# SSD output of a hybrid SSD/MLA step: y scaled group by group, and the order of three GpSimd products in two scan groups

## The chip, the cores and the metric

The kernel runs on one core of one Trainium2 chip. The metric is device time in microseconds (us). The core has five engines that work side by side, each through its own instructions in order: TensorE (PE in the profile; its weight loads are listed as PEld), VectorE (DVE), ScalarE (ACT), GpSimd (POOL) and SyncE (SP), which issues most of the transfers. They wait for each other by semaphores.

## The reference

One step of a two-layer decoder trunk: a Mamba-2 SSD layer, then a latent-attention layer, over a prompt of 1024 tokens and 8 × 8 sample tokens. The change lies in the SSD layer. There a projection gives z, x, B, C and dt; x, B and C go through a causal convolution and SiLU; then come the chunked scan, the skip product, the gate, a normalisation over each of 8 groups of 256 channels, and the output projection:

```python
def ssd_scan(x, dt, a_head, bm, cm, init_state):
    ...
    y_diag = jnp.einsum('bgrcls,bcsgrp->bclgrp', cb[:, :, None] * decay, xdt)
    decay_end = jnp.exp(a_cs[..., -1:] - a_cs).transpose(0, 3, 4, 1, 2)
    states = jnp.einsum('bcsgn,bcsgrp->bcgrpn', bc, xdt * decay_end[..., None])
    ...
    def step(s, inp):
        st, dec = inp
        return dec[..., None, None] * s + st, s
    ...
    y_off = jnp.einsum('bclgn,bcgrpn->bclgrp', cc, prev) * decay_in[..., None]

def ssd_mixer(...):
    ...
    y = y + d_skip.astype(F32)[:, None] * xs
    y = y.reshape(b, t, SSD_D_INNER) * jax.nn.silu(z.astype(F32))
    yg = y.reshape(b, t, SSD_GROUPS, SSD_D_INNER // SSD_GROUPS)
    yg = yg * lax.rsqrt(jnp.mean(yg * yg, axis=-1, keepdims=True) + NORM_EPS)
    y = yg.reshape(b, t, SSD_D_INNER) * norm_w.astype(F32)
    out = jnp.einsum('bte,ed->btd', y.astype(h.dtype), w_out)
```

## The kernel before

All numbers are float32. To keep their precision on TensorE, most operands are split in two: a high part, which ACT makes by a rounding copy, and a low part, the **remainder**, value minus high part, which DVE or POOL makes. A product is then three matmuls (high × high, high × low, low × high). `split` (L125) issues the two instructions; its subtraction is on POOL where POOL is passed, and it returns that last instruction.

**Groups.** The SSD layer goes over the 8 channel groups. While group g is scanned (`ssd_scan`, L733, which interleaves `ssd_chunks` and `ssd_states`), the projection, convolution and gate of group g+1 are issued beside it (L926 to L938). The last group, g = 7, has no next group: beside its scan stands the first half of the output projection (L949 to L953).

**A chunk.** `ssd_chunks` (L580) takes nine tiles of tokens, eight chunks of 128 prompt tokens and one of 64 sample tokens. For each prompt chunk:
- PE transposes x and B; ACT copies x out as xsT.
- POOL multiplies xsT by the decay to the chunk's end: xdd (L613). `split` makes xddh (ACT) and xddl (POOL, L615, listed under L133).
- From the second chunk on, C and the state S are split too (L617 to L620).
- POOL multiplies xsT by the skip weight: xD (L622).
- The 128x512 matrix M of decays is loaded by SP (L626), masked on DVE (L627), exponentiated on ACT (L630) and multiplied by C·B on DVE (L631); PE multiplies it with xsT into py (L635).
- PE adds Bh·xddh, Bh·xddl, Bl·xddh into st (L639), in that order; from C and S it makes the state's part of py (L644).
- POOL decays the state, S2 = S × decay (L645); DVE adds st to it (L647).
- DVE and POOL join y from py, xD (L653) and z; ACT squares it into xD, whose buffer is reused (two buffers); SP stores y (L658).

**The states of the sample.** `ssd_states` (L669) treats the 8 × 8 sample tokens; its line L713 splits a transposed state, and the remainder, called sl, is made on DVE and used by PE at L719.

**The output projection.** `OutHalf.prep` (L801) loads one tile of y with four groups (1024 columns), multiplies each group's 256 columns by that group's norm factor (L812), transposes it on PE (L820) four blocks at a time, and splits it. `ssd_out` (L832) does the matmuls. The first half (tiles named yta, poa; groups 0 to 3) runs beside the scan of group 7; the second (ytb, pob; groups 4 to 7) after it. There are nine tiles in each half.

**What sets the order.** In this layer the program gives the dependences, and a planner orders each engine's instructions at build time by a timeline of its own; an engine then works through its list strictly in order. `k.tc.issue_after(ins)` makes the instructions traced in its block, on the same engine as `ins`, stand behind `ins` in that list. The attention layer's PE and POOL lists are written out by hand (`manual_schedule`, L1999 and L2003). Transfers on SP's queue are in order too.

Of the kernel before, what the change touches and what calls it, by code (L numbers as in the profile page):

```python
# [11 lines left out]
ALU = mybir.AluOpType  # L12
# [15 lines left out]
G = 8  # L28
# [54 lines left out]
def mm3(nc, out, pairs):  # L83
    n = len(pairs)
    for i, (a, b) in enumerate(pairs):
        nc.tensor.matmul(out, a, b, start=(i == 0), stop=(i == n - 1))  # L86
# [38 lines left out]
def split(k, hi, lo, src, eng=None, parts=0):  # L125
    nc = k.nc
    nc.scalar.copy(hi, src)  # L127
    n = parts and hi.shape[1] // parts
    for a in range(parts):
        s = slice(a * n, a * n + n)  # L130
        (eng or nc.vector).tensor_tensor(lo[:, s], src[:, s], hi[:, s].bitcast(F32), op=ALU.subtract)
    if not parts:
        return (eng or nc.vector).tensor_tensor(lo, src, hi.bitcast(F32), op=ALU.subtract)  # L133
# [446 lines left out]
def ssd_chunks(k, gr, pools):  # L580
    nc, I = k.nc, k.I
    sp, psum = pools
    g = gr.g
    S = None
    hs = slice(4 * g, 4 * g + 4)
    for i in range(9):
        t0, m = TILES[i]
        sl = slice(t0, t0 + m)
        smp = i == 8
        B, C, X0, X1 = (gr.xc[q][1][:, j] if smp else gr.xc[q][0][:, j, sl] for q in range(2) for j in range(2))  # L590
        z = gr.z[i // 5][:m, i % 5]
        tag = f"{g}_{i}"
        p = psum.tile([128, 512], F32, tag="tr", name="trp" + tag, bufs=PB["tr"])
        nc.tensor.transpose(p[:m, 0:128], X0, k.ident)
        nc.tensor.transpose(p[:m, 128:256], X1, k.ident)
        if not smp:
            nc.tensor.transpose(p[:m, 256:384], B, k.ident)
        xsT = sp.tile([128, 256], F32, tag="xsT", name="xsT" + tag, bufs=2)
        nc.scalar.copy(xsT[:m], p[:m, 0:256])  # L599
        if not smp:  # L600
            Bh, Bl = (sp.tile([128, 128], F32R, tag="BT" + x, name="BT" + x + tag, bufs=2) for x in "hl")
            split(k, Bh, Bl, p[:, 256:384])
        tk = k.tok[:m, i]

        def hb(j):
            return tk[:, j, hs].unsqueeze(2).to_broadcast([m, 4, 64])

        def v3(t):
            return t[:m].rearrange("p (h q) -> p h q", q=64)

        if not smp:
            xdd = sp.tile([128, 256], F32, tag="xdd", name="xdd" + tag, bufs=1)
            nc.gpsimd.tensor_tensor(v3(xdd), v3(xsT), hb(2), op=ALU.mult)  # L613
            dh, dl = (sp.tile([128, 256], F32R, tag="xdd" + x, name="xdd" + x + tag, bufs=1) for x in "hl")
            split(k, dh, dl, xdd, nc.gpsimd)  # L615
            if S is not None:
                Ch, Cl = (sp.tile([128, 128], F32R, tag="C" + x, name="C" + x + tag, bufs=1) for x in "hl")  # L617
                split(k, Ch, Cl, C, nc.gpsimd)
                Sh, Sl = (sp.tile([128, 256], F32R, tag="S" + x, name="S" + x + tag, bufs=1) for x in "hl")
                split(k, Sh, Sl, S, nc.gpsimd)  # L620
        xD = sp.tile([128, 256], F32, tag="xD", name="xD" + tag, bufs=XDB)
        nc.gpsimd.tensor_tensor(v3(xD), v3(xsT), k.dsk[:m, hs].unsqueeze(2).to_broadcast([m, 4, 64]), op=ALU.mult)  # L622
        pc = psum.tile([128, 512], F32, tag="cb", name="cb" + tag, bufs=PB["cb"])
        nc.tensor.matmul(pc[:m, :m], B, C, start=True, stop=True)
        M = sp.tile([128, 4, 128], F32, tag="M", name="M" + tag, bufs=2)
        nc.sync.dma_start(M[:m, :, :m], (k.acss_d[hs] if smp else k.acs_d[i, hs]).partition_broadcast(m))  # L626
        nc.vector.tensor_tensor(M[:m, :, :m], M[:m, :, :m],  # L627
                                (k.negs if smp else k.negu)[:m, :m].unsqueeze(1).to_broadcast([m, 4, m]), op=ALU.add)
        for h in range(4):
            nc.scalar.activation(M[:m, h, :m], M[:m, h, :m], AF.Exp, bias=tk[:, 0, 4 * g + h : 4 * g + h + 1])  # L630
        nc.vector.tensor_tensor(M[:m, :, :m], M[:m, :, :m],  # L631
                                pc[:m, :m].unsqueeze(1).to_broadcast([m, 4, m]), op=ALU.mult)
        py = psum.tile([128, 512], F32, tag="y", name="py" + tag, bufs=PB["y"])
        for h in range(4):
            nc.tensor.matmul(py[:m, h * 64 : h * 64 + 64], M[:m, h, :m], xsT[:m, h * 64 : h * 64 + 64],  # L635
                             start=True, stop=True)
        if not smp:
            ps = psum.tile([128, 512], F32, tag="st", name="st" + tag, bufs=PB["st"])
            mm3(nc, ps[:, :256], [(Bh, dh), (Bh, dl), (Bl, dh)])  # L639
            S2 = sp.tile([128, 256], F32, tag="S", name=f"S{g}_{i + 1}", bufs=2)  # L640
            if S is None:
                nc.vector.tensor_copy(S2, ps[:, :256])
            else:
                mm3(nc, py[:m, 256:], [(Ch, Sh), (Ch, Sl), (Cl, Sh)])  # L644
                nc.gpsimd.tensor_tensor(S2.rearrange("p (h q) -> p h q", q=64), S.rearrange("p (h q) -> p h q", q=64),  # L645
                                        k.decp[:, hs, i : i + 1].to_broadcast([128, 4, 64]), op=ALU.mult)
                nc.vector.tensor_tensor(S2, S2, ps[:, :256], op=ALU.add)  # L647
            S = S2
        y = sp.tile([128, 256], F32, tag="y", name="y" + tag, bufs=YB)
        if i:  # L650
            nc.vector.tensor_tensor(v3(y), v3(gr.yo if smp else py[:, 256:]), hb(3), op=ALU.mult)
            nc.vector.tensor_tensor(y[:m], y[:m], py[:m, :256], op=ALU.add)
            nc.gpsimd.tensor_tensor(y[:m], y[:m], xD[:m], op=ALU.add)  # L653
        else:
            nc.vector.tensor_tensor(y, py[:, :256], xD, op=ALU.add)
        nc.vector.tensor_tensor(y[:m], y[:m], z, op=ALU.mult)
        nc.scalar.activation(xD[:m], y[:m], AF.Square, accum_out=k.yssq[:m, i, g : g + 1])
        nc.sync.dma_start(k.y_d[sl, 256 * g : 256 * g + 256], y[:m])  # L658
        if i == 7:
            pf = psum.tile([128, 512], F32, tag="tr", name="pf" + tag, bufs=PB["tr"])  # L660
            for pr in range(2):
                nc.tensor.transpose(pf[:, pr * 128 : pr * 128 + 128], S[:, pr * 128 : pr * 128 + 128], k.ident)
            fo = sp.tile([128, 256], F32, tag="fo", name="fo" + tag, bufs=1).rearrange("p (a n) -> p a n", a=2)
            nc.scalar.copy(fo, pf[:, :256].rearrange("p (a n) -> p a n", a=2))
            nc.sync.dma_start(k.O["p_ssm"][0, 0, 4 * g : 4 * g + 4].rearrange("(a h) p n -> (h p) a n", h=2), fo)
        yield
# [129 lines left out]
class OutHalf:  # L796
# [4 lines left out]
    def prep(self, i, yp, psum):  # L801
        k, nc, tag, k0 = self.k, self.k.nc, self.tag, self.k0
        nk = NWA
        g0, ng = k0 // 2, nk // 2
        if self.rs is None:
            self.rs = k.cs.tile([128, 9, ng], F32, name="yrs" + tag)
            rstd_of(k, self.rs, k.yssq[:, :, g0 : g0 + ng], 256)
        t0, m = TILES[i]
        y = yp.tile([128, ng, 256], F32, tag="yt", name=f"yt{tag}{i}", bufs=1)
        nc.sync.dma_start(y[:m].rearrange("p g c -> p (g c)"),  # L810
                          k.y_d[t0 : t0 + m, k0 * 128 : (k0 + nk) * 128])
        nc.vector.tensor_tensor(y[:m], y[:m], self.rs[:m, i].unsqueeze(2).to_broadcast([m, ng, 256]), op=ALU.mult)  # L812
        yh = yp.tile([128, nk, 128], F32R, tag="yh", name=f"yh{tag}{i}", bufs=1)
        yl = yp.tile([128, nk, 128], F32R, tag="yl", name=f"yl{tag}{i}", bufs=1)
        yv = y.rearrange("p g c -> p (g c)")
        for q in range(nk // 4):
            p = psum.tile([128, 512], F32, tag="tr", name=f"ytp{tag}{i}{q}", bufs=PB["tr"])
            for a in range(4):
                b = q * 4 + a
                nc.tensor.transpose(p[:, a * 128 : a * 128 + m], yv[:m, b * 128 : b * 128 + 128], k.ident[:m, :m])  # L820
            pv = p.rearrange("p (a t) -> p a t", a=4)[:, :, :m]
            qs = slice(q * 4, q * 4 + 4)
            split(k, yh[:, qs, :m], yh[:, qs, 64:] if m == 64 else yl[:, qs], pv)
        return yh, yl
# [1240 lines left out]
```

## Time and profile before

| what | value |
|---|---|
| three runs | 1943.63, 1947.31, 1948.73 us (median 1947.31) |
| profiled execution | 1942.63 us, its span 1940.9 us |
| granted TensorE clock in it | 0.995 of full speed |
| HBM read and written | 146.52 MB and 53.28 MB |

The profile is of one execution. Rows of a group of instructions give line, engine, operation, output <- inputs, shapes and count, then busy time and mean duration in ns of one, then the idle time of the engine before them and what ended it. Rows of a timeline start with the start in us and the duration in us; in brackets stands the idle time before, with what ended it. Rows of waits give the waiting engine and line, the producer, and total, number and longest. Rows of windows give the length of the stretch, the busy time and number of instructions of each engine, the granted clock, and the share and rate of DMA. A buffer's number is left out of its name, so that xddl is one of several. Matmuls overlap one another: their starts, not their durations, show the rate.

The scale of y takes 1212 to 2876 ns in the first half of the output projection (median 1464, nine instructions) and 1215 to 1227 ns in the second (nine). xD is made 72 times (606 to 1687 ns, median 615), the remainder xddl 64 times (727 to 2266, median 741), the decayed state 56 times (614 to 1803, median 623).

### The profile page before, as it was taken

The page shows a single profiled execution, that of the slowest core. Times are in us where ns is not written, and L with a number is a line of the kernel's source. Part 1 is how long each engine was busy: PE and PEld are TensorE (multiplying, and loading weights), DVE is VectorE, ACT ScalarE, POOL GpSimd, SP SyncE. Part 2 cuts the span into 40 slices and gives each one's busy share as a digit, 9 for nine tenths or more (in the row PEclk, how much of TensorE's full clock was granted, in tenths as well). Part 3 has the DMA queues.
Part 4 walks back from the last instruction along what each step waited for, and adds up shares of the span by engine and source line. Part 5 has one row for each costly group of instructions (what it writes and reads, how often), then busy time and mean ns, then how long its engine had stood idle before and what let it go on. Part 6 is the DMA issues. An engine that isn't in the chain of part 4 may idle for free.

```text
span 1940.9 us, 33581 instructions
## 1 busy us (share of the span) xinstructions
PE 1896.4 (98%) x12023; PEld 1731.9 (89%) x12023; DVE 1191.3 (61%) x2447; ACT 1110.6 (57%) x2535; POOL 844.3 (44%) x1122
## 2 busy tenths in 40 slices
PE   9999999999999999899999999999999999999998
PEld 7999999999999999788787998898888888778887
DVE  5557565756665666765533104466787878676674
ACT  6466676666667676743214314335777777855552
POOL 2447455555655555444003213203443434774551
PEclk9999999999999999999999999999999999999999
DMA  5123323332333332553533333132111112654441
GB/s 165 50 72 87 92 84 98 82 110 82 93 89 93 83 99 66 189 180 133 197 124 109 134 141 91 64 109 89 55 52 41 52 41 59 205 177 154 155 128 39
DMA packets 181087, 202.02 MB, mean 104 GB/s; under 512 B 18828, under 2 KB 147608, under 8 KB 180536
## 3 DMA queue, kind: packets, MB, share of 16 engines
q1 hardware_dynamic: 175864, 180.08, 30.3%
q0 software_dynamic: 4976, 19.66, 3.0%
q8 instruction: 95, 1.56, 0.3%
q14 instruction: 72, 0.59, 0.1%
q10 hardware_dynamic: 80, 0.13, 0.0%
HBM read 146.52 MB, written 53.28 MB: 103 GB/s over the span
## 4 chain that ended last, share of the span: by engine, by line
PE 85%; ACT 4%; DVE 3%; DMA 3%; POOL 2%; issue 1%; SPq 0%; POOLq 0%; DVEq 0%; ACTq 0%
PE pj L86 21%; PE pz L98 8%; PE pq L98 6%; PE pob L98 5%; PE p L98 5%; PE poa L98 5%; PE py L635 2%; PE sc L86 2%; PE o L86 2%; PE sc L1365 2%; PE o L1428 2%; PE o L1430 2%; PE st L1397 2%; PE st L1398 2%; PE st L1399 2%; PE o L1429 2%
## 5 line engine op out<-in xcount | busy, mean ns | idle before, releaser
L86 PE MATMUL pj<-xh,wih 128*128 128x384 f32 (+1 forms) x768 | 254.7, 336 | 0.5 <-ACT raw L512 0.3
L86 PE MATMUL pj<-xl,wih 128*128 128x384 f32 (+1 forms) x768 | 254.1, 331 | 0.0
L86 PE MATMUL pj<-xh,wil 128*128 128x384 f32 (+1 forms) x768 | 253.6, 330 | 0.0
L1411 POOL TENSOR_TENSOR tl<-P,th 128x384 fp32r<-128x384 f32 (+1 forms) x96 | 90.6, 944 | 232.5 <-ACT P L1409 190.9
L526 DVE SCALAR_TENSOR_TENSOR acc<-raw,vec,acc 128x1112 f32<-128x1112 f32 x96 | 141.6, 1476 | 26.5 <-ACT acc L522 25.5
L86 PEld LDWEIGHTS pj<-xh,wih 128*128 128x128 f32 x768 | 144.3, 189 | 2.2 <-ACT xh L273 0.7
L86 PEld LDWEIGHTS pj<-xl,wih 128*128 128x128 f32 x768 | 144.9, 189 | 1.0
L86 PEld LDWEIGHTS pj<-xh,wil 128*128 128x128 f32 x768 | 144.7, 188 | 0.4
L98 PE MATMUL pz<-wih,xh 128*128 128x256 f32 x504 | 142.8, 287 | 0.5 <-ACT z L567 0.5
L98 PE MATMUL pz<-wil,xh 128*128 128x256 f32 (+1 forms) x504 | 140.2, 284 | 0.0
L1408 ACT ACTIVATE th<-st 128x512 fp32r<-128x512 f32 x192 | 94.6, 493 | 65.9 <-PE st L1404 50.3
L98 PE MATMUL pz<-wih,xl 128*128 128x256 f32 x448 | 128.2, 286 | 0.0
L630 ACT ACTIVATE M<-M,tok 128x128 f32<-128x128 f32 (+1 forms) x288 | 90.9, 386 | 64.2 <-DVE M L627 63.8
L1701 POOL TENSOR_TENSOR kvl<-pgr,kvh 128x256 fp32r<-128x256 f32 x128 | 97.6, 789 | 57.4 <-ACT kvh L1699 57.0
L98 PEld LDWEIGHTS pz<-wih,xh 128*128 128x128 f32 x504 | 95.9, 190 | 1.3 <-ACT z L567 0.9
L1409 ACT ACTIVATE P<-st 128x512 f32<-128x512 f32 x192 | 93.5, 487 | 0.0
L98 PEld LDWEIGHTS pz<-wil,xh 128*128 128x128 f32 (+1 forms) x504 | 92.7, 184 | 0.7
L627 DVE TENSOR_TENSOR M<-M,negu 128x512 f32<-128x512 f32 x64 | 50.6, 790 | 67.2 <-DMA M<-acs_d 67.1
L133 DVE TENSOR_TENSOR wil<-wraw,wih 128x512 fp32r<-128x512 f32 x88 | 72.2, 828 | 25.8 <-ACT wih L127 22.7
L98 PEld LDWEIGHTS pz<-wih,xl 128*128 128x128 f32 x448 | 85.3, 190 | 0.1
L613 POOL TENSOR_TENSOR xdd<-xsT,tok 128x256 f32<-128x256 f32 x64 | 50.2, 784 | 80.7 <-ACT xsT L599 80.3
L1411 DVE TENSOR_TENSOR tl<-P,th 128x512 fp32r<-128x512 f32 x96 | 70.8, 737 | 18.9 <-ACT P L1409 18.0
(832 smaller groups left out, 6308.3 us busy)
## 6 DMA issues: line engine op xcount, KB each, us to landing
wraw<-in_ssd_w_in SPq DMA_DIRECT2D x92, 256.0 KB
M<-acs_d SPq DMA_DIRECT2D x64, 256.0 KB
s<-in_state_ssm SPq DMA_DIRECT2D x32, 256.0 KB
y_d<-y SPq DMA_DIRECT2D x64, 128.0 KB
out_s_ssm<-s SPq DMA_DIRECT2D x32, 256.0 KB
wraw<-in_ssd_w_out SPq DMA_DIRECT2D x12, 512.0 KB
q_d<-qt SPq DMA_DIRECT2D x32, 192.0 KB
qp<-q_d SPq DMA_DIRECT2D x8, 768.0 KB
```

The costliest lines, as they stand in the source:

```text
L86: nc.tensor.matmul(out, a, b, start=(i == 0), stop=(i == n - 1))
L98: nc.tensor.matmul(o, a, b, start=(j == 0), stop=(j == len(ops) - 1))
L133: return (eng or nc.vector).tensor_tensor(lo, src, hi.bitcast(F32), op=ALU.subtract)
L526: last = nc.vector.scalar_tensor_tensor(acc, raw[:, j : j + n], k.convw[j][:, blk : blk + 1], acc, op0=ALU.mult, op1=ALU.add)
L613: nc.gpsimd.tensor_tensor(v3(xdd), v3(xsT), hb(2), op=ALU.mult)
L627: nc.vector.tensor_tensor(M[:m, :, :m], M[:m, :, :m], (k.negs if smp else k.negu)[:m, :m].unsqueeze(1).to_broadcast([m, 4, m]), op=ALU.add)
L630: nc.scalar.activation(M[:m, h, :m], M[:m, h, :m], AF.Exp, bias=tk[:, 0, 4 * g + h : 4 * g + h + 1])
L635: nc.tensor.matmul(py[:m, h * 64 : h * 64 + 64], M[:m, h, :m], xsT[:m, h * 64 : h * 64 + 64], start=True, stop=True)
L1408: nc.scalar.activation(th[:, :n], ps[:, :n], AF.Exp, scale=SCALE)
L1409: nc.scalar.activation(P[:, :n], ps[:, :n], AF.Exp, scale=SCALE)
L1411: eng.tensor_tensor(tl[:, :n], P[:, :n], th[:, :n].bitcast(F32), op=ALU.subtract)
L1701: nc.gpsimd.tensor_tensor(rl[:, j], raw[:, j], rh[:, j].bitcast(F32), op=ALU.subtract)
```

## The change

It has two parts.

In `ssd_chunks`, the remainder's instruction that `split` returns is kept as `behind`. In the groups 0 and 7, xD (except that of the sample tile) and the decayed state S2 are traced under `issue_after(behind)`: on POOL they stand behind the remainder xddl of the same chunk. In the other groups nothing is added.

In `OutHalf.prep`, the one product of 1024 columns with the norm factors spread over each group (`tensor_tensor`, two inputs) becomes four products of 256 columns, each with one column of factors as a per-partition scalar (`tensor_scalar`). It applies to both halves of the output projection, to all nine tiles.

```diff
-            split(k, dh, dl, xdd, nc.gpsimd)
+            behind = split(k, dh, dl, xdd, nc.gpsimd)
...
-        nc.gpsimd.tensor_tensor(v3(xD), v3(xsT), k.dsk[:m, hs].unsqueeze(2).to_broadcast([m, 4, 64]), op=ALU.mult)
+        with k.tc.issue_after(behind.ins) if not smp and g in (0, G - 1) else nullcontext():
+            nc.gpsimd.tensor_tensor(v3(xD), v3(xsT), k.dsk[:m, hs].unsqueeze(2).to_broadcast([m, 4, 64]), op=ALU.mult)
...
-                nc.gpsimd.tensor_tensor(S2.rearrange("p (h q) -> p h q", q=64), S.rearrange("p (h q) -> p h q", q=64),
-                                        k.decp[:, hs, i : i + 1].to_broadcast([128, 4, 64]), op=ALU.mult)
+                with k.tc.issue_after(behind.ins) if g in (0, G - 1) else nullcontext():
+                    nc.gpsimd.tensor_tensor(S2.rearrange("p (h q) -> p h q", q=64),
+                                            S.rearrange("p (h q) -> p h q", q=64),
+                                            k.decp[:, hs, i : i + 1].to_broadcast([128, 4, 64]), op=ALU.mult)
...
-        nc.vector.tensor_tensor(y[:m], y[:m], self.rs[:m, i].unsqueeze(2).to_broadcast([m, ng, 256]), op=ALU.mult)
+        for g in range(ng):
+            nc.vector.tensor_scalar(y[:m, g], y[:m, g], self.rs[:m, i, g : g + 1], None, op0=ALU.mult)
```

## The prediction

> **What bounds the kernel now.** I read the page first, then the stages by windows, then who waited for whom, and last the timelines of PE, POOL, DVE, ACT and SP around the two longest waits that this change can touch.
>
> ```profile
> span 1940.9 us, 33581 instructions
> PE 1896.4 (98%) x12023; PEld 1731.9 (89%) x12023; DVE 1191.3 (61%) x2447; ACT 1110.6 (57%) x2535; POOL 844.3 (44%) x1122
> ```
>
> The reader is to see that PE is never without work for long: 1940.9 − 1896.4 = 44.5 us of idle time is all that can be won without fewer matmuls, plus what a lowered clock costs. So each edit is worth what it takes from PE's waits, and nothing for the time of DVE or POOL as such. Next the stages: the first scan group runs at about 117 to 215 us, groups 1 to 6 to 800, and the last one from 800 to 925, beside the first half of the output projection.
>
> ```profile
> core 0: us, PE busy (x) PEld busy (x) DVE busy (x) ACT busy (x) POOL busy (x), PEclk, DMA share, GB/s
> 117.00:215.00 98.00, 93.22 (x689) 91.07 (x688) 66.93 (x109) 65.27 (x166) 63.37 (x90) 0.98 0.33 94
> 215.00:800.00 585.00, 579.51 (x4258) 567.26 (x4257) 378.90 (x629) 396.41 (x970) 330.19 (x481) 1.00 0.32 92
> 800.00:830.00 30.00, 24.31 (x142) 20.31 (x141) 24.99 (x38) 21.30 (x48) 14.82 (x20) 0.94 0.76 250
> 830.00:925.00 95.00, 94.82 (x528) 79.81 (x528) 52.95 (x94) 31.13 (x90) 40.80 (x51) 1.00 0.46 155
> ```
>
> PE's idle time sits in the first scan group (98 − 93.2 = 4.8 us) and in the first 30 us of the last one (5.7 us); in the 585 us between it is 5.5 us, and from 830 to 925 it is 0.2 us. PE's list of waits, longest in total first, begins with this row:
>
> ```profile
> PE st L86 <- POOL xddl L133: 3.6, 2, 2.5
> ```
>
> The remainder xddl was late twice; the timeline of PE places the two, one in each of the groups that the change names. Here is the longer wait for xddl: rows of PE, ACT, POOL and DVE.
>
> ```profile
> 159.31 0.36 PE L86 MATMUL st<-xddh,BTh 128*128 128x256 f32 x1
> 162.15 0.58 PE L86 MATMUL st<-xddl,BTh 128*128 128x256 f32 x1 [2.48 <-POOL xddl L133]
> 165.20 0.34 PE L86 MATMUL pj<-xh,wil 128*128 128x384 f32 x1
> 157.10 0.40 ACT L127 CAST xddh<-xdd 128x256 fp32r<-128x256 f32 x1
> 157.28 1.41 POOL L622 TENSOR_TENSOR xD<-xsT,dsk 128x256 f32<-128x256 f32 x1 [1.58 <-ACT xD L657]
> 158.65 1.69 POOL L645 TENSOR_TENSOR S<-S,decp 128x256 f32<-128x256 f32 x1
> 160.30 1.79 POOL L133 TENSOR_TENSOR xddl<-xdd,xddh 128x256 fp32r<-128x256 f32 x1
> 156.84 4.67 DVE L526 SCALAR_TENSOR_TENSOR acc<-raw,vec,acc 128x1112 f32<-128x1112 f32 x3 [0.48 <-ACT acc L522]
> ```
>
> xddh was ready at 157.10 + 0.40 = 157.50, but POOL did xD and the decayed state first, each stretched by DVE's three long instructions beside them, and began xddl at 160.30. This is exactly the order that the change forbids.
>
> **Edit 1: xddl ahead of xD and decayed state, first group.** Nothing is added; two POOL instructions are moved behind one, in every chunk of the two groups. At this wait xddl can begin at 157.5. Stretched as it was it takes 1.79 and is done at 159.3, when PE has just issued the matmul on xddh (159.31); the wait of 2.48 goes. A second term goes with it:
>
> ```profile
> 157.40 0.33 PE L86 MATMUL pj<-xh,wih 128*128 128x384 f32 x1
> 157.57 0.33 PE L86 MATMUL pj<-xl,wih 128*128 128x384 f32 x1
> 160.00:165.00 5.00, 2.85 (x10) 2.85 (x11) 3.64 (x6) 0.00 (x0) 5.00 (x9) 0.67 0.00 2
> 820.00:825.00 5.00, 4.94 (x24) 4.24 (x25) 5.00 (x9) 2.90 (x6) 0.00 (x0) 0.66 0.39 79
> 825.00:830.00 5.00, 3.41 (x20) 2.71 (x19) 4.35 (x8) 3.95 (x13) 4.48 (x6) 1.00 0.89 328
> ```
>
> Before the wait a matmul of 384 columns starts every 0.17 us; the ten that start from 162.15 up to 165.20 took 3.05 us, against 10 × 0.17 = 1.7: 1.3 us lost to the granted clock (0.67 in that window). Together 2.5 + 1.3 = **3.8 us**. Late next is the decayed state: behind xddl (159.3) and xD (1.41) it ends at 159.3 + 1.4 + 1.7 = 162.4 instead of 160.34. The DVE add that takes it waited for PE's st matmuls, the last of which began after 162.15, so the recurrence is no later than before. POOL's sum of work to that point is unchanged, so what is queued behind (the remainders of C and of S, then y's add of xD) ends when it did, while PE is 3.8 us earlier; bounds for this term are therefore 0 (PE then waits for those) and 3.8. I take 3.8, because the two operands that PE lacked are the only ones named in its waits there.
>
> **The same edit in the last group.**
>
> ```profile
> 826.09 0.40 ACT L127 CAST xddh<-xdd 128x256 fp32r<-128x256 f32 x1
> 826.58 1.71 POOL L133 TENSOR_TENSOR xddl<-xdd,xddh 128x256 fp32r<-128x256 f32 x1
> 829.51 0.74 POOL L133 TENSOR_TENSOR xddl<-xdd,xddh 128x256 fp32r<-128x256 f32 x1
> 826.24 1.46 DVE L812 TENSOR_TENSOR yta<-yta,yrsa 128x1024 f32<-128x1024 f32 x1 [0.65 <-DMA yta<-y_d]
> 828.35 0.39 PE L86 MATMUL st<-xddl,BTh 128*128 128x256 f32 x1 [1.09 <-POOL xddl L133]
> ```
>
> Here xddh was ready at 826.49 and xddl began at 826.58, so the order alone is worth 0.1 us. What made it late was the scaling of y on DVE: xddl took 1.71 where the next one took 0.74. With the scaling in four pieces, one piece of some 0.3 us (below) stands before xddl: 826.5 + 0.3 + 0.74 = 827.5, 0.8 earlier than 828.29. [...] The clock stayed at 1.00 after this wait (window from 825), so there is no second term.
>
> **Edit 2: y scaled in four pieces.** 18 instructions of 128x1024 (two inputs) become 72 of 128x256 (one input and a column).
>
> ```profile
> L812 DVE TENSOR_TENSOR ytb<-ytb,yrsb 128x1024 f32<-128x1024 f32 x8 | 9.8, 1222 | 10.1 <-DMA ytb<-y_d 8.7 <-POOL yrsb L224 1.4
> L236 DVE TENSOR_SCALAR xt<-xrb,hrs 128x1024 f32<-128x1024 f32 x6 | 4.5, 754 | 4.0 <-POOL hrs L224 4.0
> L219 DVE TENSOR_SCALAR yrsb<-yssq 128x36 f32<-128x36 f32 x1 | 0.2, 182 | 0.0
> ```
>
> The new form in its 128x256 shape isn't in the trace. From the two rows of that operation: (754 − 182) / (1024 − 36) = 0.58 ns a column, so 182 + 220 × 0.58 = 0.31 us, and four take 1.24 us against 1.22. Bounds: 4 × 0.18 = 0.7 (nothing but the short row's time) and 4 × (1.22 / 4 + 0.18) = 1.9 (each column as slow as now, and that time on top). On DVE that is +0.4 us over 18 tiles, from −9 to +12 at the bounds, and DVE is idle for 95 − 53 = 42 us from 830 to 925 alone, while PE idles 0.2; so I put it at 0 on the path. If that cover were gone, it would cost those 0.4 us.
>
> What counts is the place where the long instruction stood before a critical one:
>
> ```profile
> 816.53 2.88 DVE L812 TENSOR_TENSOR yta<-yta,yrsa 128x1024 f32<-128x1024 f32 x1
> 819.33 0.68 DVE L133 TENSOR_TENSOR sl<-s0p,sh 128x512 fp32r<-128x512 f32 x1
> 820.06 0.31 PE L719 MATMUL pv<-sl,cblk 128*32 128x128 f32 x2 [2.45 <-DVE sl L133]
> 817.60 0.72 POOL L133 TENSOR_TENSOR Sl<-S,Sh 128x256 fp32r<-128x256 f32 x1
> ```
>
> The scaling started at 816.53 and lasted 2.88 where it takes 1.22 alone: POOL's work to 817.60 + 0.72 = 818.32 held it up, and sl stood behind it. If sl can go after one piece or before the pieces, it starts at about 818.3 instead of 819.33: 1.0 less waiting. The remaining wait of 1.45 is less than the 1.59 that PE idled from 825 to 830, in two waits, while the clock was 1.00; so the slow stretch also goes, 5 × (1 − 0.66) = 1.7 us. Sum **2.7 us**. Bounds: 0 (sl stays behind all four pieces) and 2.45 + 1.7 = 4.15. I take 2.7, between the two.
>
> [...]
>
> **Sum.** 3.8 + 0.8 + 2.7 = 7.3 us, less nothing: the profiled span would go from 1940.9 to 1933.6. The page's execution is one of the quicker ones (1942.63 beside its span of 1940.9, against the median of 1947.31 in three runs), so I set the change against the median: 1947.3 − 7.3 = **1940.0**. What is won early lasts, since PE is busy 579.5 of the following 585 us.
>
> **Rivals.** *The order is right, but little of it reaches the end (22%).* The order on each engine outside the hand-ordered part is planned at build time; the pieces may stay together ahead of sl, and in the first group PE may run into the next operand (bounds above: 0 for each). One half of the first group's 3.8, 1.9, plus 0.8: 1947.3 − 2.7 = 1944.6. For it: PE's idle time in the first group is 4.8, not much more than what is claimed. Against: no other wait on PE within 5 us of that place.
>
> *Slower by what is held back (20%).* POOL works in order. Until now it did xD and the decayed state while ACT was still making xddh; now both stand behind xddl, and y's add, y's store and what is behind that store on SP's queue wait for them.
>
> ```profile
> POOL xddl L133 <- ACT xddh L127: 4.2, 3, 2.8
> SPq L658 <- DVE y L656: 18.8, 6, 9.2
> 188.67 0.39 PE L86 MATMUL py<-Sl,Ch 128*128 128x256 f32 x1
> 187.89 0.72 POOL L133 TENSOR_TENSOR Sl<-S,Sh 128x256 fp32r<-128x256 f32 x1
> 165.41 0.34 SPq L658 DMA_DIRECT2D y_d<-y  x1
> 168.27 0.84 SPq L626 DMA_DIRECT2D M<-acs_d  x2
> L622 POOL TENSOR_TENSOR xD<-xsT,dsk 128x256 f32<-128x256 f32 (+1 forms) x10 | 7.3, 732 | 4.4 <-ACT xD L657 4.2 <-ACT xsT L599 0.2
> ```
>
> In the first group SP already waited 18.8 us to store y, and the next loads of M follow that store (165.41, 168.27); PE took one Sl 0.06 us after POOL ended it (188.61). If xD alone (0.73 in the mean of this stage) now comes after the wait in each of 16 chunks, POOL gives 16 × 0.73 = 11.7 us, and all of it is PE's where there is no slack; with the gain of 3.8 gone too and 2.7 + 0.8 kept: 1947.3 + 11.7 − 3.5 = 1955.5. It decides once POOL's wait for xddh in a group grows beyond the 34.6 us (98 − 63.4) that POOL is free. Against it: that room.
>
> *Slower by a new plan elsewhere (10%).* An altered order early in the program can alter that of later groups, untouched by the edits. Three new waits like the one at 162, at 3.8 each, would cost 11.4 − 7.3 = +4; five, +11.7: 1951 to 1959. For it: 5.5 us idle in 585 leaves much to lose. Against: those groups' instructions and dependences are the same.
>
> **How the numbers follow.** The forecast has 48%: 1940.0, its own range 1935 (all upper bounds: 3.8 + 1.09 + 4.15 = 9.0, and 3 us for the median) to 1944. The whole range, **1932 to 1957**, takes in a plan that comes out some 6 us better, the rivals on the slow side, and the runs' spread of 5.1 us. What a measurement here can tell from no change is about 0.3%, 5.8 us. Faster beyond that: most of the forecast's share, **0.45**; within: its lesser part and the first rival, **0.25**; slower: **0.30**.
>
> **What would show it.** In the profile after: POOL's rows in both groups in the order xdd, xddl, xD, in all chunks; no PE wait of over 1 us for xddl; the clock at 1.00 from 160 to 165; pieces of 0.31 us on L812's successor; sl ahead of some piece. Wrong would be: new PE waits for Sl, M or the state in the first group, PE idle time in groups 1 to 6 well over 5.5 us, or POOL waiting much over 4.2 us for xddh.

## The result, and the profile after

| series | before, median (runs) | changed, median (runs) | ratio, 95% interval |
|---|---|---|---|
| first | 1946.31 us (20) | 1942.76 us (20) | 0.9981 (0.9973 to 0.9990) |
| second | 1948.28 us (25) | 1943.37 us (12) | 0.9974 (0.9962 to 0.9986) |

The change is faster by 0.19% and 0.26%: 3.6 us by the first series' medians, 4.9 us by the second's. Both intervals lie below 1, and the size is still under the 0.3% that the prediction set as its bound for "faster". The forecast was 1940.0, 7.3 us below before. The direction came out; of the size, a half to two thirds did.

Here are the head of the page after and the stages by windows (columns as in the prediction).

```profile
span 1939.4 us, 33638 instructions
PE 1895.6 (98%) x12023; PEld 1730.3 (89%) x12023; DVE 1192.2 (61%) x2501; ACT 1109.9 (57%) x2535; POOL 837.5 (43%) x1122
```

```profile
117.00:215.00 98.00, 95.75 (x709) 92.74 (x707) 69.51 (x114) 68.21 (x175) 64.93 (x93) 1.00 0.34 101
215.00:800.00 585.00, 579.11 (x4264) 566.46 (x4263) 379.16 (x632) 394.50 (x964) 326.93 (x480) 1.00 0.32 91
800.00:830.00 30.00, 25.31 (x131) 20.35 (x130) 24.05 (x44) 19.35 (x45) 13.83 (x18) 0.94 0.74 252
830.00:925.00 95.00, 95.00 (x534) 80.10 (x534) 53.96 (x112) 32.48 (x93) 37.88 (x49) 1.00 0.49 166
```

PE's busy time in the first scan group rose from 93.2 to 95.75 of 98 us and its clock from 0.98 to 1.00. In the first 30 us of the last group it rose by 1.0 us only, with the same mean clock, 0.94. From 215 to 800 us nothing moved. The profiled span is 1.5 us shorter than the one before, though the medians differ by more: 1940.9 was one of the quicker executions of the kernel before.

The first scan group after, from the timelines of POOL, ACT and PE (start, duration, engine, instruction, idle time ahead of it):

```profile
155.00 0.40 ACT L127 CAST xddh<-xdd 128x256 fp32r<-128x256 f32 x1
155.48 1.83 POOL L133 TENSOR_TENSOR xddl<-xdd,xddh 128x256 fp32r<-128x256 f32 x1 [0.53 <-ACT xddh L127]
157.27 1.68 POOL L623 TENSOR_TENSOR xD<-xsT,dsk 128x256 f32<-128x256 f32 x1
157.36 0.39 PE L86 MATMUL st<-xddl,BTh 128*128 128x256 f32 x1 [0.35 <-POOL xddl L133]
158.91 1.69 POOL L647 TENSOR_TENSOR S<-S,decp 128x256 f32<-128x256 f32 x1
```

POOL now makes xddl as soon as xddh is there, and PE's wait of 2.48 us is down to 0.35. The same view of the last group, PE and DVE:

```profile
802.33 0.50 PE L98 MATMUL poa<-xh,yha 128*128 128x512 f32 x1 [1.51 <-ACT yha L127]
...
814.06 2.03 DVE L816 TENSOR_SCALAR yta<-yta,yrsa 128x256 f32<-128x256 f32 x4
816.02 0.68 DVE L133 TENSOR_TENSOR sl<-s0p,sh 128x512 fp32r<-128x512 f32 x1
816.75 0.31 PE L722 MATMUL pv<-sl,cblk 128*32 128x128 f32 x2 [1.13 <-DVE sl L133]
820.94 0.50 PE L98 MATMUL poa<-xl,yha 128*128 128x512 f32 x1 [0.94 <-DVE xl L770]
823.60 0.38 PE L86 MATMUL st<-xddl,BTh 128*128 128x256 f32 x1 [0.24 <-POOL xddl L133]
824.57 0.39 PE L86 MATMUL st<-xddh,BTl 128*128 128x256 f32 x1 [0.58 <-DVE BTl L133]
```

The wait for sl fell from 2.45 to 1.13 and that for xddl from 1.09 to 0.24. But the four pieces stand together ahead of sl (one row, x4), not around it, and two operands that were in time before, xl and BTl, are now late by 0.94 and 0.58: a part of the gain is handed on to them. For xl it is the clock's part: the kernel with the order in group 0 alone, whose last group is as before, waits 0.95 for xl too, in an execution without the slow stretch at 820. The granted clock in 5 us windows of that place:

```profile
800.00:805.00 5.00, 3.49 (x18) 2.69 (x17) 3.35 (x7) 4.92 (x12) 1.40 (x4) 0.78 0.99 343
805.00:810.00 5.00, 5.00 (x22) 3.98 (x21) 3.65 (x5) 3.16 (x7) 3.23 (x3) 0.88 0.95 347
820.00:825.00 5.00, 2.95 (x15) 2.14 (x15) 4.93 (x10) 3.46 (x13) 3.64 (x5) 1.00 0.94 320
```

The slow stretch that stood at 820 (0.66) is gone, and another stands at 800 to 810, behind the wait of 1.51 for yha. It costs 5 × (0.22 + 0.12) = 1.7 us, exactly the term that the prediction took as won.

### The profile page after: what moved, and what is told of

It reads as the page before. It is cut to its first block, busy times and chain, and to the rows that moved or that the text cites. A ratio compares the mean times of both kernels' runs of the same rounds, so it can differ in the third digit from the quotient of the medians.

```text
span 1939.4 us, 33638 instructions
## 1 busy us (share of the span) xinstructions
PE 1895.6 (98%) x12023; PEld 1730.3 (89%) x12023; DVE 1192.2 (61%) x2501; ACT 1109.9 (57%) x2535; POOL 837.5 (43%) x1122
## 4 chain that ended last, share of the span: by engine, by line
PE 88%; DVE 3%; DMA 3%; ACT 3%; issue 1%; POOL 1%; SPq 0%; POOLq 0%; DVEq 0%; ACTq 0%
PE pj L86 21%; PE pz L98 9%; PE pq L98 6%; PE pob L98 5%; PE p L98 5%; PE poa L98 4%; PE py L636 3%; PE sc L86 3%; PE o L86 2%; PE sc L1369 2%; PE o L1432 2%; PE o L1434 2%; PE st L1401 2%; PE st L1402 2%; PE st L1403 2%; PE o L1433 2%
```

## The experiments

Ten kernels, with 5 to 12 runs each, in three sets on three chips: the first four rows, the next four and the last two. Each set has one series of the kernel before beside it (35, 25 and 23 runs), so a series that came out high or low would move all ratios of its set alike.

| kernel | median, us | ratio to before | 95% interval |
|---|---|---|---|
| order alone, groups 0 and 7 | 1943.77 | 0.9980 | 0.9969 to 0.9991 |
| pieces alone | 1945.19 | 0.9984 | 0.9975 to 0.9993 |
| order alone, group 0 | 1945.49 | 0.9984 | 0.9973 to 0.9994 |
| order alone, group 7 | 1945.33 | 0.9983 | 0.9971 to 0.9995 |
| the change again | 1943.37 | 0.9974 | 0.9962 to 0.9986 |
| change, tile 2's pieces behind sl | 1942.77 | 0.9974 | 0.9960 to 0.9988 |
| change, order in all eight groups | 1969.39 | 1.0108 | 1.0092 to 1.0124 |
| change, pieces in two-input form | 1949.86 | 1.0009 | 0.9997 to 1.0021 |
| change, xD alone held back | 1947.15 | 0.9998 | 0.9985 to 1.0011 |
| change, decayed state alone held back | 1945.45 | 0.9983 | 0.9972 to 0.9995 |

To place gains inside a run, the start of the same matmul was compared with the profile of the kernel before. The table shows how that difference moved within a stretch (us; minus is time won).

| kernel | 150 to 250 (rest of group 0) | 250 to 800 (groups 1 to 6) | 800 to 950 (group 7) |
|---|---|---|---|
| change, first profile | −2.45 | +0.64 | −0.44 |
| change, again | −2.41 | +4.60 | −1.81 |
| order, groups 0 and 7 | −0.91 | +3.07 | −1.85 |
| order, group 0 | −0.90 | +2.35 | −0.79 |
| order, group 7 | +0.75 | +5.07 | −2.56 |
| pieces alone | +0.87 | +5.95 | −1.71 |
| tile 2's pieces behind sl | −1.79 | +4.70 | +2.99 |
| pieces in two-input form | −2.49 | +5.79 | +2.21 |
| xD alone held back | +0.23 | +1.25 | −1.19 |
| state alone held back | +0.19 | +1.79 | −0.67 |

How far one execution can be trusted is read from rows with unaltered work. From about 240 us to 800 the order of the instructions is that of before in all of these but for the pieces of one tile (below), and still the difference moves by 0.6 to 6 us, always upward: the profiled execution of before was lucky there. In group 0, pieces alone and order in group 7 alone change nothing and show +0.87 and +0.75. In group 7, order in group 0 alone changes nothing and shows −0.79. So a single stretch of some 100 us is good to about 1 us, and the middle stretch is not evidence for anything under 6.

The stage of the first group begins earlier, at 117 us. From there to 250 the change won 3.2 us in each of its two profiles, the order in both groups 1.5 and the order in group 0 alone 2.1; the two kernels that leave the group as it was moved by +0.6 and −0.5.

One more thing goes with the edit: inside a group that has the new order the planner also ordered the other engines anew. In the first group of the change, up to 237 us, the orders of PE, DVE and ACT differ from before in 34 to 45 places each. No run separates this from POOL's order.

### The order alone, in both groups

```diff
+            behind = split(k, dh, dl, xdd, nc.gpsimd)
+        with k.tc.issue_after(behind.ins) if not smp and g in (0, G - 1) else nullcontext():
+                with k.tc.issue_after(behind.ins) if g in (0, G - 1) else nullcontext():
...
         nc.vector.tensor_tensor(y[:m], y[:m], self.rs[:m, i].unsqueeze(2).to_broadcast([m, ng, 256]), op=ALU.mult)
```

> Edit 1 alone, in both groups; y scaled in one instruction as before. Theory (what was won came from the order in the first group, little from the rest): the transposes of the first group's state, at 204.3 us before, come 3 to 4.5 us earlier, no wait of PE for xddl over 0.5 us there, clock 1.00 from 160 to 165; in the last group the wait for xddl stays at 0.7 to 1.1 us, since the long scaling still holds POOL up. Whole time -3 to -4.5 us, ratio 0.9977 to 0.9985. Rival (the pieces gave the gain): at most -1.5 us, ratio above 0.999.

PE's waits in the last group:

```profile
PE poa L98 <- ACT yha L127: 1.5, 1, 1.5
PE pv L722 <- DVE sl L133: 1.2, 1, 1.2
...
PE st L86 <- POOL xddl L133: 0.8, 1, 0.8
```

0.9980. The wait for sl went from 2.45 to 1.2 with the long scaling still in place, so it isn't the pieces that bring this. The wait for xddl kept 0.8 of its 1.09. In the first group the wait and the clock came out as expected, the gain did not: the place at 204 us came 2.5 us earlier, not 3 to 4.5.

### The pieces alone

```diff
-        nc.vector.tensor_tensor(y[:m], y[:m], self.rs[:m, i].unsqueeze(2).to_broadcast([m, ng, 256]), op=ALU.mult)
+        for g in range(ng):
+            nc.vector.tensor_scalar(y[:m, g], y[:m, g], self.rs[:m, i, g : g + 1], None, op0=ALU.mult)
```

> Edit 2 alone: four pieces, the order of POOL as before. Theory: the first group is as before (wait of 2.5 us for xddl, slow clock behind it); in the last group the wait for xddl of 1.1 us falls to 0.2 to 0.5, the one for sl of 2.45 stays above 1.5, because the four pieces stand together ahead of sl in DVE's list; whole time 0 to -2 us, ratio 0.999 to 1.000. Rival (the pieces gave the gain): -3 us or more, ratio 0.9985 or less, with the wait for sl below 1.2 us.

PE's waits in the last group:

```profile
PE pv L719 <- DVE sl L133: 2.3, 1, 2.3
...
PE st L86 <- DVE BTl L133: 0.5, 1, 0.5
...
PE st L86 <- POOL xddl L133: 0.2, 1, 0.2
```

The mirror image: sl stays late by 2.3, xddl is in time (0.2), and BTl, which now stands behind four pieces on DVE, is late by 0.5. In the last group the two edits thus act on different waits: **the order on sl, the pieces on xddl**, where the prediction had given sl to the pieces. The ratio of 0.9984 (3.1 us) is more than the 0 to 2 us expected, and more than the saved waits explain.

### The order in one group at a time

```diff
-  ... if not smp and g in (0, G - 1) else nullcontext()
+  ... if not smp and g == 0 else nullcontext()
```

and the same with `g == G - 1`.

> Edit 1 in the first group only, y scaled as before. Theory: all of the first group's gain, -3.8 us by the prediction's own term, ratio 0.998; the last group's lists as before, its waits of 1.1 and 2.45 us too. Rival (what is held back costs as much as is won): the state's transposes come less than 2 us earlier than 204.3, with new waits of PE for Sl, M or the state, ratio above 0.999.

> Edit 1 in the last group only, y scaled as before. Theory: the order alone is worth 0.1 us at the wait for xddl (it began 0.1 us after its operand was ready), and up to 0.6 us at sl, because the decayed state no longer runs beside the long scaling; time within 1 us of before, ratio 0.9993 to 1.0003. Rival (the last group's gain is the order's): -1.2 us or more at the last transposed tile of the first half (926.4 us before), wait for xddl under 0.4 us.

0.9984 and 0.9983: each group by itself is worth about 3 us, and both together 0.9980. The expectation for the last group (within 1 us of before) missed the 3.0 us measured; its wait for sl fell to 1.2, more than the 0.6 that was expected at most. In the first group the wait for xddl went in both kernels that have the order there, but the clock, in windows of the kernel with the order in group 0 alone, did this:

```profile
160.00:165.00 5.00, 4.78 (x36) 4.46 (x36) 3.65 (x7) 0.77 (x2) 4.40 (x8) 1.00 0.01 2
170.00:175.00 5.00, 3.56 (x22) 3.00 (x21) 4.27 (x9) 4.88 (x17) 2.36 (x4) 0.90 0.28 76
175.00:180.00 5.00, 5.00 (x35) 4.95 (x35) 4.63 (x6) 1.92 (x4) 3.65 (x3) 0.76 0.61 169
```

The slow stretch of 160 to 165 has moved to 170 to 180, behind a wait of 1.1 for wil; it costs 5 × (0.10 + 0.24) = 1.7 us. In both profiles of the change those windows are at 1.00, after the same instructions. That is about the difference between −0.9 and −2.4 in the second table.

### The change again, and with sl ahead of the pieces

```diff
-            split(k, sh, sl_, pt)
+            k.slsub = split(k, sh, sl_, pt)
...
+        with k.tc.issue_after(k.slsub.ins) if (k0, i) == (0, 2) else nullcontext():
+            for g in range(ng):
+                nc.vector.tensor_scalar(y[:m, g], y[:m, g], self.rs[:m, i, g : g + 1], None, op0=ALU.mult)
```

> The whole change once more, unaltered, beside the next three on one chip. Each edit alone, and the first edit in one group alone, came out at a ratio of 0.998 (3 us), and so did the whole change (0.9981). Theory: the whole is worth about 3.5 us whatever it is made of, because the slow stretches of the clock that follow a wait are not removed but move to the next wait: ratio 0.9975 to 0.9988; PE's wait for xddl under 0.5 us in the first scan group, for sl about 1.1 and for xddl about 0.25 in the last; some stretch of 5 us under a clock of 0.9 in 150 to 230 or 800 to 830, at a place other than in the first profile. Rival: what the single edits bring adds up, 3 + 3 us, ratio 0.997 or less, no such stretch in either group.

> The whole change, with the four pieces of tile 2 put behind sl in DVE's order, as the prediction assumed that they would stand. Theory: sl then starts when sh is ready, at about 816.1 of the change's own profile, and PE's wait for sl falls from 1.1 to 0.5 us or less; but the pieces, and with them y's transposes, come 0.7 us later and the next operands in line (xl, BTl, xddl) take what was won: 0 to 1 us below the change itself (ratio 0.9970 to 0.9988 against the kernel before), with a wait for yt or yh behind it. Rival, the prediction's step: the sl wait was worth 2.7 us, of which the change got only some; another 1.5 us or more below the change itself, no new wait above 0.5.

The second kernel does by hand what the prediction assumed of the planner. Its PE waits in the last group:

```profile
PE poa L98 <- DVE xl L770: 1.7, 2, 1.0
PE st L86 <- ACT xddh L127: 1.1, 1, 1.1
```

sl is gone from the list, and the time is that of the change, 0.9974 both. xl takes over 0.8 of it and xddh another 0.8 (it was 0.3 in the change). So no gain from the rest of the wait for sl shows at the end: PE meets the next late operand. The +2.99 of this kernel in the second table comes from its clock, 0.82 and 0.50 in the two windows from 825 to 835, which is 3.4 us, and a third slow stretch from 807.7 (0.77 from 805 to 810), another 1.7. The change itself had 1.00 in all windows from 800 to 850 in its second profile: its expected slow stretch (the theory's "some stretch under 0.9") did not show up in either group.

### The order in all eight groups

```diff
-        with k.tc.issue_after(behind.ins) if not smp and g in (0, G - 1) else nullcontext():
+        with k.tc.issue_after(behind.ins) if not smp else nullcontext():
...
-                with k.tc.issue_after(behind.ins) if g in (0, G - 1) else nullcontext():
+                with k.tc.issue_after(behind.ins):
```

> The whole change, with POOL's order (xddl ahead of xD and of the decayed state) in all eight scan groups instead of two. Theory: in groups 1 to 6 PE does not wait for xddl (5.5 us of idle time in 585 in all), and POOL has 255 us free there, so that nothing is won or lost: within 1.5 us of the change itself, PE's busy time from 215 to 800 still about 579. Rival, the prediction's case of what is held back: xD and the decayed state behind the wait for xddh cost POOL 0.7 us in each of 48 chunks, and PE where it has no slack: 5 us slower than the change or more, with waits for y, Sl or M in those groups.

1.0108: 26 us slower than the change on the same chip. The theory was wrong, and the rival had the direction. PE's longest waits from 215 to 800 us, then POOL and PE at one of them:

```profile
PE pv L722 <- ACT sh L127: 8.5, 6, 2.2
PE py L86 <- POOL Sl L133: 7.0, 6, 1.3
PE sn L729 <- DVE S L643: 5.0, 5, 1.8
```

```profile
257.88 0.73 POOL L133 TENSOR_TENSOR xddl<-xdd,xddh 128x256 fp32r<-128x256 f32 x1
258.58 1.68 POOL L623 TENSOR_TENSOR xD<-xsT,dsk 128x256 f32<-128x256 f32 x1
260.23 1.53 POOL L133 TENSOR_TENSOR Cl<-acc,Ch 128x128 fp32r<-128x128 f32 x1
261.72 0.61 POOL L647 TENSOR_TENSOR S<-S,decp 128x256 f32<-128x256 f32 x1
262.30 0.72 POOL L133 TENSOR_TENSOR Sl<-S,Sh 128x256 fp32r<-128x256 f32 x1
263.07 0.39 PE L86 MATMUL py<-Sl,Ch 128*128 128x256 f32 x1 [1.26 <-POOL Sl L133]
```

xD and the decayed state used to fill POOL's time until xddh was there. Held behind xddl they stand in front of Cl and Sl, and PE comes for Sl before POOL has made it. In the first profile of the change these three waits sum to 1.3 + 0.3 + 0.3 = 1.9 us in that stretch, here to 20.5; two slow stretches there (mean clock 0.83 from 320 to 330 and from 685 to 695) cost 1.7 us each. The planner ordered the other engines anew in these groups too, so POOL's order alone is not shown to cost all 26 us. The change is a gain only because it leaves six groups alone.

### The pieces in two-input form

```diff
-            nc.vector.tensor_scalar(y[:m, g], y[:m, g], self.rs[:m, i, g : g + 1], None, op0=ALU.mult)
+            nc.vector.tensor_tensor(y[:m, g], y[:m, g], self.rs[:m, i, g : g + 1].to_broadcast([m, 256]), op=ALU.mult)
```

> The whole change, with y scaled in four pieces still, but each by the two-input form that the kernel before used on all 1024 columns. It separates the cutting from the one-column form. Theory: the one-column form is what keeps the pieces short beside POOL's work; two-input pieces take about 0.35 us each alone (1.4 for four) and are held up beside POOL like the one long instruction (2.9 us for four beside POOL's scaling, against 2.0 now): PE's wait for sl in the last group about 2 us or more, or that for xddl back at 0.7; 0 to 1 us slower than the change. Rival: the cut alone does it, since POOL's work can go between pieces: waits as in the change (1.1 and 0.25).

1.0009 against 0.9974: the form matters more than either theory gave it, 6.5 us. The waits for sl (1.9) and xddl (0.2) in the last group are near those of the change. The loss stands at two places of about the same size. One is the last group all the same, +2.21 in the second table against −0.44 and −1.81: new waits of 1.1 for b and 1.0 for yla, and a slow stretch at 820 to 830 (0.88 and 0.78). The other is the scaling of the first tile, the one that runs beside group 4. DVE in this kernel, in the change again, and in the kernel before, where POOL's row stands with it:

```profile
514.00 5.52 DVE L816 TENSOR_TENSOR yta<-yta,yrsa 128x256 f32<-128x256 f32 x4 [0.70 <-POOL yrsa L224]
519.45 0.27 DVE L725 TENSOR_TENSOR yo<-yo,pv 32x128 f32<-32x128 f32 x1
```

```profile
515.05 3.77 DVE L816 TENSOR_SCALAR yta<-yta,yrsa 128x256 f32<-128x256 f32 x4 [0.72 <-POOL yrsa L224]
```

```profile
516.83 2.06 DVE L812 TENSOR_TENSOR yta<-yta,yrsa 128x1024 f32<-128x1024 f32 x1 [0.69 <-POOL yrsa L224]
517.77 2.02 POOL L701 TENSOR_TENSOR bb<-b,blk 96x512 fp32r<-96x512 f32 x1
```

All three start when POOL's chain of products starts too. The one long instruction was through in 2.06, and POOL's bb beside it took 2.02, against 1.1 to 1.2 in the other two. In four pieces it took 3.77 in the one-column form and 5.52 in the two-input form. In the change's first profile, where the four took 3.77 too, they took 1.13, 1.71, 0.82 and 0.34 one by one, and the first three ended 0.14 to 0.15 us after POOL's s, decayed state and Sl did. In the two-input kernel PE then waits 2.0 for yo, behind the pieces, and the clock is at 0.66 there:

```profile
520.00:525.00 5.00, 5.00 (x21) 4.97 (x21) 4.96 (x7) 0.00 (x0) 0.11 (x1) 0.66 0.55 161
```

From 500 to 550 us this kernel lost 4.0 us against before, the change in its second profile 0.4.

### One of the two held back

```diff
-                with k.tc.issue_after(behind.ins) if g in (0, G - 1) else nullcontext():
+                with nullcontext():
```

for xD alone, and the same for the other `with`, for the decayed state alone.

> The whole change, but only xD is held behind xddl in the two groups; the decayed state is free again. Theory: in the last group the decayed state returns to its place just ahead of Sl on POOL, beside the scaling of tile 2, and the four pieces there take over 2.5 us and PE's wait for sl is back at 2 us or more (it was 2.30 with the pieces alone); in the first group the wait for xddl is back in part, by the 1.7 us of the decayed state (1 to 2 us, if the planner puts the state ahead of xddl there): 1 to 3 us slower than the change, ratio 0.998 to 1.000 against the kernel before. Rival: xD is what counts and the state's place does not: as the change, 0.9974 to 0.9981, sl 1.6 or less.

> The whole change, but only the decayed state is held behind xddl in the two groups; xD is free again. Theory: PE's wait for sl stays at 1.1 to 1.6 us, since the state is what left POOL's row of work beside the scaling; xddl in the first group waits for xD's 1.4 us alone and PE for xddl about 0.7 to 1.5 us (2.48 before, 0.35 now): within 1.5 us of the change, ratio 0.9974 to 0.9988. Rival: xD ahead of xddl is what made it late, so the first group's wait is back at 2 us or more and the time 2 to 3 us above the change, 0.999.

0.9998 and 0.9983. Timelines of POOL and DVE in the last group, of the kernel that holds back xD alone:

```profile
816.92 1.27 POOL L704 TENSOR_TENSOR bb<-b,blk 96x512 fp32r<-96x512 f32 x1 [0.72 <-DVE b L702]
817.67 2.73 DVE L816 TENSOR_SCALAR yta<-yta,yrsa 128x256 f32<-128x256 f32 x4
818.16 0.62 POOL L647 TENSOR_TENSOR S<-S,decp 128x256 f32<-128x256 f32 x1
818.74 0.72 POOL L133 TENSOR_TENSOR Sl<-S,Sh 128x256 fp32r<-128x256 f32 x1
```

and of the one that holds back the state alone:

```profile
817.75 2.04 DVE L816 TENSOR_SCALAR yta<-yta,yrsa 128x256 f32<-128x256 f32 x4
818.37 0.74 POOL L133 TENSOR_TENSOR Sl<-S,Sh 128x256 fp32r<-128x256 f32 x1
```

With the state between bb and Sl, POOL's three products follow each other without a gap and the pieces take 2.73; with the state gone behind xddl, 2.04. PE waits 2.3 for sl in the first and 1.6 in the second. So **the place of the decayed state** decides over some 0.7 us of the wait for sl, one profile against one. In group 0 neither alone wins anything over 150 to 250 us (+0.23, +0.19), though the wait for xddl is down to 0.4 with xD alone and to 0.7 with the state alone. With the state alone PE then waits 1.4 for b, 1.3 for yo and 0.6 each for S and xddh; with xD alone it waits 0.8 for yo, 0.7 for xddh and 0.6 for wil, and a slow stretch (0.67 from 175 to 180) takes 1.65 us. The first expectation put 1 to 2 us on xddl there, and that was wrong: the planner let the state run in the gap before xddh, and it delayed nothing.

## Why the prediction was right or wrong

The forecast's direction and main mechanism held, and the time lies between it and the first rival. By stage: of the 3.8 us booked for the first group the change's profiles show 3.2, of the 3.5 booked for the last one they show 0.4 and 1.8. The time of 1940.0 was nearer than the gain: before's median is 1946.31 over twenty runs, 1.0 below the three that the forecast started from, and that is luck.

**First group, 3.8.** The mechanism held: order, xddl at xddh's heels, the wait of 2.48 down to 0.35 and the clock at 1.00 from 160 to 165. The size is 3.2 in both profiles of the change. The prediction said that "no other wait on PE within 5 us of that place" spoke for the full term; the waits stand further on, at wil (0.8 to 1.6 over the profiles with this order), yo (0.4) and sl (up to 0.3), and catch PE when it arrives early.

**The clock terms, 1.3 and 1.7.** The first one held in the change; the second is the step that failed. (In the first, two of the ten matmuls have 256 columns, which start every 0.12 us, so its size is nearer to 1.4.) Three executions keep the wait of 2.5 for xddl in the first group, and all three have a slow stretch behind it; nine have it shortened, and none is slow at 160 to 165, though three of them are at 174 to 178. In the last group four executions keep a wait of 2.3 to 2.5 for sl: before has the slow stretch, the other three (pieces alone, order in group 0, xD alone) have none near it. Of the eight with that wait shortened, six have a slow stretch somewhere from 800 to 839.

The prediction read a slow stretch behind a wait of 2.45 and none behind 1.59, and took it that shorter waits bring none. Here is that same wait for sl in before (the first two rows) and in the kernel with the order in group 0 alone:

```profile
817.02:820.43 3.41, 0.87 (x7) 0.56 (x8) 3.41 (x3) 2.62 (x4) 1.30 (x3) 1.00 0.26 75
820.43:823.85 3.42, 3.42 (x14) 2.94 (x13) 3.42 (x5) 2.41 (x4) 0.00 (x0) 0.50 0.29 69
815.68:819.09 3.41, 2.13 (x12) 1.39 (x10) 3.32 (x5) 2.72 (x7) 2.54 (x3) 1.00 0.86 236
819.09:822.50 3.41, 1.96 (x16) 1.79 (x17) 3.41 (x5) 2.13 (x4) 0.00 (x0) 1.00 0.03 9
```

In the profiles of before and of the change the granted clock, from 5 to 1936 us, stood at 1.00 but for three stretches each at 0.50. In before they run from 161.66 to 165.07, 820.43 to 823.85 and 1690.83 to 1701.07, in the change from 802.77 to 806.18, 1697.06 to 1703.89 and 1710.72 to 1714.13. Each lasts one, two or three steps of 3.41 us, and their starts lie whole numbers of such steps apart (820.43 − 161.66 = 193 × 3.413, 1697.06 − 802.77 = 262 × 3.413). In before the wait (817.6 to 820.06) lay within the one step ahead of the slow stretch, PE was busy for 0.87 us of that step, and the next one ran at 0.50, which costs 3.41 / 2 = 1.7. In the other kernel the clock stayed at 1.00 behind the wait of 2.46. Counted on in steps of 3.41 from its slow stretch at 174, a step would end at 819.09, inside that wait; this is an estimate from the steps in the two profiles above. PE was busy for 2.13 and 1.96 on the two sides. There is no sharp limit in these numbers: the change's first profile had PE busy for 1.90 of the 3.41 us ahead of its slow stretch at 802.77, and its second for 1.81 of the 3.41 us from 818.34 without one. So in these executions a wait's length alone does not decide, and a slow stretch in one profile can't be booked as the gain of removing that wait.

Nor is all of a slow stretch won where it goes: without the slow stretch PE waits 0.94 for xl. Over all runs, the mean granted clock is 0.9944 in 83 of before and 0.9950 in 32 of the change: 0.0006 × 1945 = 1.2 us (interval 0.3 to 2.0) where 3.0 were booked. Without its two clock terms the prediction's sum was 4.3, between the two sizes measured (3.6 and 4.9); that doesn't speak for leaving both out, since the first group did win its clock term and the last one little of either.

**sl in the last group, 2.7.** The wait fell by 1.3 and 0.9 in the two profiles of the change, near the 1.0 of the prediction, but for another reason. The step "if sl can go after one piece or before the pieces" failed: the planner kept the four together ahead of sl. Pieces alone left 2.3; the order alone left 1.2. The prediction had the cause in its own rows, POOL's work to 818.32 that held the scaling up, and gave the cure to the wrong edit: the decayed state (817.02 in before) was part of that row of work, and edit 1 takes it away. It then counted nothing for edit 1 at this place. With sl put first by hand the time stayed at 0.9974. How little is left of this term at the end shows in the second table: −0.44 and −1.81 for the whole group, beside −0.79 in the kernel that leaves it as it was.

**xddl in the last group, 0.8.** Right in size (1.09 to 0.24) and in cause: the pieces alone give it, the order alone only 0.3.

**Cost of the pieces, 0.** In the second half of the projection a piece takes 0.347 us in the mean, beside the estimate of 0.31, and four in a row with POOL idle take 1.13 (row in the last section); the forecast's cover held: the only wait of PE behind them is BTl's 0.6. Not foreseen: beside POOL's chain of products the scaling of the first tile took 3.77 in four one-column pieces and 5.52 in four two-input ones, against 2.06 in one instruction, which cost 0.4 us there in the one-column form and 4.0 in the two-input form.

**The rivals.** "Little of it reaches the end" (1944.6) is nearer to the 1942.76 and 1943.37 than the forecast, and its first reason, pieces that stay together, is what happened. "Slower by what is held back" did not happen in the two groups, and something like it happens in the other six: 26 us. Its point of decision was wrong, though. POOL was free for 264 of the 585 us there. The rows point to Cl and Sl, which are due right behind xddl in the same chunk; but in the first group of the change they stand behind xD and the state too (Cl at 161.20, Sl at 161.61), and PE does not wait for them. Why one place pays and the other doesn't is not shown. "A new plan elsewhere" is refuted: from 240 us on, outside the last group and the pieces, the order of instructions is unaltered on every engine.

**Open.** The order (0.9980), the pieces (0.9984) and the order in either group alone each measure about 3 us, and all together 3.6 to 4.9. With intervals of ±2 us they may add up or overlap, or their common series of before came out high; the runs don't separate this. Nor do they tell POOL's order from the planner's new order on the other engines in the first group. Why the pieces alone win 3 us when their waits in the last group account for about 1 is open too.

## What to carry to other kernels

A wait that is taken away is worth what lies up to the next late operand (here the wait for sl fell by 1.3 us in one profile, and xl came 0.94 late behind it), so list the next three waits of the waiting engine before booking it, and book no clock from a single profile: see first whether the slow stretch comes back in others. When GpSimd's order is changed, look at which VectorE instructions run beside it: moving one GpSimd product out of an unbroken row took 0.7 us off a wait on PE here. An order that helps where GpSimd lags may cost far more where it was using the time until its operand came (26 us here, in all eight groups), so it is put in group by group.

## What the hardware showed

Beside each other DVE's scaling and POOL's products took longer than apart, and not always the same one of them. The long scaling, 1.22 us in the second half of the projection, took 2.06 in the first tile, where POOL's second product beside it, bb, took 2.02 instead of 1.1 to 1.2. In the last group it took 2.88 (816.53 to 819.41), while POOL's bb, decayed state and Sl, in a row up to 818.32, took 1.27, 0.62 and 0.72. The decayed state started 0.49 us after the scaling, took its usual 0.62 and ended before it:

```profile
817.02 0.62 POOL L645 TENSOR_TENSOR S<-S,decp 128x256 f32<-128x256 f32 x1
```

Here are four one-column pieces of the change and four two-input pieces, with POOL idle beside them:

```profile
837.40 1.13 DVE L816 TENSOR_SCALAR yta<-yta,yrsa 128x256 f32<-128x256 f32 x4
```

```profile
844.85 1.42 DVE L816 TENSOR_TENSOR yta<-yta,yrsa 128x256 f32<-128x256 f32 x4
```

So four one-column pieces lost 3.77 − 1.13 = 2.6 us at the first tile, and four two-input pieces 5.52 − 1.42 = 4.1, where the one long instruction lost 2.06 − 1.22 = 0.8. In the last group, beside bb, the decayed state and Sl in a row, four one-column pieces took 2.73 (xD alone held back) and the long instruction 2.88 (before).

PE's granted clock fell to 0.78 (mean of 800 to 805) behind a wait of 1.51 us in one execution, the change's first, and stayed at 1.00 behind one of 2.46 in another, that of the order in group 0 alone. In the profiles of before and of the change each fall between 5 and 1936 us went to 0.50 and lasted 3.41 us or two or three times that, which is 1.7 us of work for each 3.41, by the clock (an estimate: 3.41 / 2).
